# Splitting plain weight blocks with casting and accumulating DMAs in a two-layer trunk kernel

## The chip, the cores and the metric

The kernel is one program on one core of a Trainium2 chip. The engines named below are PE (matrix multiplication, and PEld, its weight loads), DVE (elementwise), ACT (elementwise with functions), POOL (elementwise, and a queue of DMAs of its own) and SP (which here only issues DMAs). The metric is the device time of one execution in microseconds; the median of three runs stands for a kernel.

## The reference

A stream of 512 latent tokens and 256 context tokens, 1024 wide, goes through two layers. Layer 0 mixes tokens with a bidirectional chunkwise mLSTM, layer 1 with windowed grouped-query attention. A squared-ReLU MLP of width 4096 follows each. All in float32:

```
u = modulate(rms_norm(h, norm_mix[i]), shift, scale)
y = mixer(u, uc, w_in, w_out)                 # mLSTM (i = 0) or windowed attention (i = 1)
h = h + gate * y
h = h + gate2 * (square(relu(modulate(rms_norm(h, norm_ffn[i]), ...) @ w1[i])) @ w2[i])
return rms_norm(h, final_norm)
```

The context stream runs through layer 0 in full, and in layer 1 only as keys and values. Shifts, scales and gates come from a product of the conditioning vector with a 1024 by 6144 matrix in each layer.

## The kernel before

**Products.** TensorE gets float32 operands in its reduced type fp32r, so each operand is split into a high part (the operand cast to fp32r) and a low part (the operand less its high part). A product takes three matmuls, `mm3` at lines 96 to 98: high by high, low by high, high by low.

**Weight units.** Weights come as units of 128 by 1024 numbers (512 KB). A *plain* unit is a block as it lies in memory. `unit` (lines 73 to 87) loads it on SP's queue into one of three buffers `raw` (line 80), and `split` makes ACT cast it to `whi` (line 887) and DVE subtract to get `wlo` (line 888). `whi` and `wlo` have four buffers each, so a new unit can be split once the unit four before it has had its last matmul. I call the time from that last matmul to the first matmul of the new unit the unit's *lead*. The load lies before the lead, since `raw` is separate; the cast and the subtraction lie in it. In `dense_steps` each unit is asked for by `take`, which keeps two ahead; elsewhere `feed` takes the next of a planned list, and `take` and `feed` are placed by hand in the code of each stage.

**Stages,** in order of time: a start of some 50 us (loads, the first norms, the conditioning product), layer 0's mixer (to about 540 us; weights wg, wqk, wv, wo, wout, all plain), layer 0's MLP `ffn0` (540 to 920 us), layer 1's attention (920 to 1130 us; wskv, wsq, wsout, plain) and layer 1's MLP `ffn1` (1130 us to the end).

- `ffn0` multiplies two row blocks of w1 with halves of the tokens by a scheme of seven products instead of eight. Its w1 blocks are not plain: `pair_w1` loads two into `raw` (lines 986, 987), and POOL makes sums of them, four instructions on lines 994 to 997, which are then cast and subtracted. In `seven`, POOL also squares one result (line 1085) and adds two others (line 1088, `addg`). After each group of such products, `back` multiplies with w2, whose units (`w2a`) are plain: four to a chunk, in each of seven chunks.
- `ffn1` takes plain w1 units and forms its second product by a seven-product scheme over 2 by 2 groups of w2 blocks (`plan1`, lines 1180 to 1245): the blocks stay in tiles `wb`, and 28 subtractions on DVE (`less`, line 1208) form the sums of blocks that the scheme wants. These sums are split by the ACT cast and DVE subtraction of `split`.

The sequence on each engine is not the order of the code: a scheduler in the compiler orders the instructions of all engines by its own estimates, and the engines then run what they are given strictly in that order. A DMA issued on POOL's queue stands in POOL's order among its sums and squares: an entry that waits holds up all behind it.

POOL issues no DMA in the kernel before.

Of the kernel before, what the change touches and what calls it, by code (L numbers as in the profile page):

```python
# [9 lines left out]
F32 = mybir.dt.float32  # L10
F32R = mybir.dt.float32r
BF16 = mybir.dt.bfloat16
AF = mybir.ActivationFunctionType
ALU = mybir.AluOpType
# [7 lines left out]
P = 128  # L22
D = 1024
KT = D // P
NL = 512
# [31 lines left out]
class Trunk:  # L57
# [14 lines left out]

    def unit(self, src, eng=None):

        nc = self.nc
        if len(src.shape) == 3:
            src = src.rearrange("m p c -> p m c")
        n = int(np.prod(src.shape[1:]))
        raw = self.ring.tile([P, D], F32, name="raw", tag="raw", bufs=self.nraw)[:, :n]
        nc.sync.dma_start(out=raw if len(src.shape) == 2 else raw.rearrange("p (m c) -> p m c", m=src.shape[1]), in_=src)  # L80
        hi = self.ring.tile([P, D], F32R, name="whi", tag="whi", bufs=self.nsplit)[:, :n]
        lo = self.ring.tile([P, D], F32R, name="wlo", tag="wlo", bufs=self.nsplit)[:, :n]
        self.split(raw, hi, lo, eng)
        if self.ada_cap and self.ada_todo and self.ada_todo[0][:2] < self.ada_cap:
            self.ada_step()
        return hi, lo
# [1103 lines left out]
    def plan1(self):  # L1190

        nc, a = self.nc, self.a
        self.steps1 = [(0, 4), (8, 4), (16, 4), (24, 2)]
        self.w2r = w2r = {}
        at = 0

        def load(b, u, n):
            def f():  # L1200
                t = w2r[b, u] = self.fp.tile([P, D], F32, name=f"wb{b}", tag=f"w{b}{u}")
                nc.sync.dma_start(out=t, in_=a["w2b"][n])
            return f

        def less(o, x, y, u):

            def f():
                nc.vector.tensor_tensor(out=w2r[o, u], in0=w2r[x, u], in1=w2r[y, u], op=ALU.subtract)
            return f

        def w1(m, *extra):
            def f():
                r = self.unit(a["w1"][1, m])
                for x in extra:
                    x()
                return r
            return f

        def w2(b, u, *extra):
            def f():  # L1220
                hi, lo = [self.ring.tile([P, D], F32R, name=n, tag=n, bufs=self.nsplit) for n in ("whi", "wlo")]
                self.split(w2r[b, u], hi, lo)
                for x in extra:
                    x()
                return hi, lo
            return f
        self.plan, self.begun = [], []
        for base, nk in self.steps1:
            us = range(nk // 2)
            extra = []  # L1230
            for b in (12, 22, 11, 21):
                extra += [load(b, u, at + (11, 12, 21, 22).index(b) * len(us) + u) for u in us]
            extra += [less(12, 12, 11, u) for u in us]
            at += 4 * len(us)
            ms = [base + nk * i + k for k in range(nk) for i in range(2)]
            skip = 0 if base else 2
            per = -(-len(extra) // (len(ms) - skip))
            self.plan += [w1(m) for m in ms[:skip]]
            self.plan += [w1(m, *extra[per * i:per * i + per]) for i, m in enumerate(ms[skip:])]
            self.plan += [w2(b, u) for b in (11, 21) for u in us]  # L1240
            self.plan += [w2(22, u, less(22, 22, 12, u)) for u in us]
            self.plan += [w2(12, u, less(11, 22, 11, u)) for u in us]
            self.plan += [w2(22, u, less(21, 22, 21, u)) for u in us]
            self.plan += [w2(b, u) for b in (11, 21) for u in us]
        self.last1 = base + 2 * nk

        def w2_plain(i):

            def f():
                raw = self.ring.tile([P, D], F32, name="raw", tag="raw", bufs=self.nraw)  # L1250
                nc.sync.dma_start(out=raw, in_=a["w2l"][i])
                nc.vector.tensor_tensor(out=raw, in0=raw, in1=self.grow, op=ALU.mult)
                hi, lo = [self.ring.tile([P, D], F32R, name=n, tag=n, bufs=self.nsplit) for n in ("whi", "wlo")]
                self.split(raw, hi, lo)
                return hi, lo
            return f
        self.plan += [w1(m) for m in range(self.last1, 4 * KT)]
        self.plan += [w2_plain(i) for i in range(4 * KT - self.last1)]

    def ffn1(self, u, out):  # L1260

        nc, tc, a = self.nc, self.tc, self.a
        xs = self.xs(u)
        fp = self.fp
        H = NL // 2
        tt = nc.vector.tensor_tensor
# [27 lines left out]
        def two(name, k):  # L1294
            t = fp.tile([P, 2, NL], F32R, name=name, tag=f"{name}{k}")
            return t[:, 0, :], t[:, 1, :]
# [10 lines left out]
        def second(m, m0, k):  # L1307

            r0, r1, s34 = rt.pop(m0), rt.pop(m), rt.pop(("34", k))
            hid["12", k] = two("h12", k)  # L1310
            self.split(r1, *hid["12", k])
            s = fp.tile([P, NL], F32, name="s12", tag="s12", bufs=2)
            tt(out=s[:, 0:H], in0=r0[:, H:NL], in1=r1[:, H:NL], op=ALU.add)
            tt(out=s[:, H:NL], in0=s[:, 0:H], in1=r0[:, 0:H], op=ALU.subtract)
            tt(out=s34[:, H:NL], in0=r1[:, 0:H], in1=s[:, H:NL], op=ALU.subtract)
            for n, src in (("1", s), ("3", s34)):
                hid[n, k] = two("e" + n, k)
                self.split(src, *hid[n, k])
# [38 lines left out]
        for c, (base, nk) in enumerate(self.steps1):  # L1357
            for k in range(nk):
                m0, m1 = base + k, base + nk + k
                if c + k == 0:  # L1360
                    hidden([0, nk, 1, nk + 1], square, (("A", (0, 1)), ("A", (2, 3)), ("B", range(4))))
                if m0 not in rt:
                    hidden([m0], square)
                first(m0, k)
                if m1 not in rt:
                    hidden([m1], square)
                second(m1, m0, k)
            for p, n in ((1, "11"), (2, "12"), (3, "S4"), (5, "S1"), (6, "S2"), (7, "S3"), (4, "22")):
                if c == len(self.steps1) - 1 and p == 6:
                    self.rows1()  # L1370
                product(p, n, nk, c)
# [14 lines left out]
        def join(i):  # L1386
            a1, a3, a4, a5, a6 = [acc[p, i] for p in (1, 3, 4, 5, 6)]
            x = fp.tile([P, NL], F32, name="r", tag="r", bufs=4)
            for o, l, r, op in ((a6, a1, a6, ALU.add), (a1, kept[2, i], a1, ALU.add), (x, kept[7, i], a6, ALU.add),
                                (a6, a6, a5, ALU.add), (a3, a3, a6, ALU.add), (a4, x, a4, ALU.subtract),  # L1390
                                (a5, x, a5, ALU.add)):
                tt(out=o, in0=l, in1=r, op=op)
            for t, d, o in ((i, 0, a1), (i, 1, a3), (2 + i, 0, a4), (2 + i, 1, a5)):
                tt(out=o, in0=o, in1=self.grow[:, d * 512:(d + 1) * 512], op=ALU.mult)
                y = res[t][:, d * 512:(d + 1) * 512]
                tt(out=y, in0=y, in1=o, op=ALU.add)
        hp = []
        for n, m in enumerate(range(self.last1, 4 * KT)):
            hidden([m], square)
            hp.append(two("h12", n))  # L1400
            self.split(rt.pop(m), *hp[n])
            turn((0, 2, 1, 3)[n])
            if n % 2:
                join(n // 2)
# [3 lines left out]
        for t in (0, 2, 1, 3):  # L1408
            sv = ss[:, 3 * t:3 * t + 3]
            os = [None, None]  # L1410
            for d in range(2):
# [5 lines left out]
                y = res[t][:, ds]  # L1417
                tt(out=y, in0=ps, in1=y, op=ALU.add)
                nc.scalar.activation(out=junk[d], in_=y, func=AF.Square, accum_out=sv[:, d:d + 1])
                o = os[d] = fp.tile([P, NL], F32, name="r", tag="r", bufs=4)  # L1420
# [584 lines left out]
```

## Time and profile before

| | |
|---|---|
| median of three runs | 1549.54 us (1549.34 to 1550.19) |
| the profiled execution, its whole time | 1551.29 us |
| its span, first to last instruction | 1549.4 us |
| busy: PE, DVE, ACT, POOL | 1509.6, 1127.1, 740.2, 326.5 us |
| moved by DMA | 157.27 MB |
| mean granted TensorE clock | 0.992 |

The page gives busy time, share of the span and number of instructions for each engine, groups of equal instructions with their mean duration, and for each kind of DMA the median time from issue to landing. A row of a timeline is start, duration, engine, line, operation, output and input names, and in brackets the idle time before it with what ended that. In a row of windows come the window, its length, the busy time (and count) of PE, PEld, DVE, ACT and POOL, the granted clock, the share of time that DMA engines worked, and GB/s. The names whi, wlo, raw are those of the unit; mm, p, pb, pc, pj, kept and acc are PE's results; h and r are the MLP's activations.

### The profile page before, as it was taken

The page shows a single profiled execution, that of the slowest core. Times are in us where ns is not written, and L with a number is a line of the kernel's source. Part 1 is how long each engine was busy: PE and PEld are TensorE (multiplying, and loading weights), DVE is VectorE, ACT ScalarE, POOL GpSimd, SP SyncE. Part 2 cuts the span into 40 slices and gives each one's busy share as a digit, 9 for nine tenths or more (in the row PEclk, how much of TensorE's full clock was granted, in tenths as well). Part 3 has the DMA queues.
Part 4 walks back from the last instruction along what each step waited for, and adds up shares of the span by engine and source line. Part 5 has one row for each costly group of instructions (what it writes and reads, how often), then busy time and mean ns, then how long its engine had stood idle before and what let it go on. Part 6 is the DMA issues. An engine that isn't in the chain of part 4 may idle for free.

```text
span 1549.4 us, 23838 instructions
## 1 busy us (share of the span) xinstructions
PE 1509.6 (97%) x9110; PEld 1355.9 (88%) x9110; DVE 1127.1 (73%) x2084; ACT 740.2 (48%) x1501; POOL 326.5 (21%) x318
## 2 busy tenths in 40 slices
PE   6999999999999999999999999999999999999998
PEld 4778888878889999999999999888887988888886
DVE  3684657488797888767676667778888875757697
ACT  4533343344573332524424355666666665545454
POOL 0322111113203222232224221243443100000000
PEclk8999999999999999999999999999999999999999
DMA  8422323234231343343443422011111424150321
GB/s 316 139 83 69 125 82 118 73 116 150 74 110 42 120 139 124 125 146 125 148 145 100 150 69 66 32 34 42 42 41 43 177 83 149 41 163 28 109 69 55
DMA packets 47848, 157.27 MB, mean 102 GB/s; under 512 B 5327, under 2 KB 8911, under 8 KB 47607
## 3 DMA queue, kind: packets, MB, share of 16 engines
q1 hardware_dynamic: 46560, 154.25, 30.3%
q8 instruction: 72, 1.18, 0.3%
q10 hardware_dynamic: 1175, 1.51, 0.3%
q14 instruction: 41, 0.34, 0.1%
HBM read 153.64 MB, written 2.10 MB: 101 GB/s over the span
## 4 chain that ended last, share of the span: by engine, by line
PE 79%; DVE 6%; issue 4%; ACT 4%; POOL 3%; DMA 1%; POOLq 0%; DVEq 0%; ACTq 0%
PE mm L96 17%; PE mm L97 16%; PE mm L98 16%; PE p L98 2%; PE p L97 2%; PE p L96 2%; PE pt L1825 2%; PE pj L96 1%; PE pj L97 1%; PE pj L98 1%; PE at L843 1%; DVE adap L262 1%; PE av L1840 1%; ACT whi L887 1%; DVE wlo L888 1%
## 5 line engine op out<-in xcount | busy, mean ns | idle before, releaser
L888 DVE TENSOR_TENSOR wlo<-raw,whi 128x1024 fp32r<-128x1024 f32 (+2 forms) x152 | 179.6, 1186 | 82.3 <-ACT whi L887 80.6
L887 ACT CAST whi<-raw 128x1024 fp32r<-128x1024 f32 (+2 forms) x155 | 154.0, 999 | 141.9 <-PE mm L97 77.4
L96 PE MATMUL mm<-uH,whi 128*128 128x512 f32 (+1 forms) x496 | 189.4, 386 | 0.0
L97 PE MATMUL mm<-uL,whi 128*128 128x512 f32 (+1 forms) x496 | 186.7, 378 | 0.7 <-DVE uL L332 0.4
L98 PE MATMUL mm<-uH,wlo 128*128 128x512 f32 (+1 forms) x496 | 186.9, 378 | 0.0
L262 DVE SCALAR_TENSOR_TENSOR adap<-raw,crow 128x1024 bf16<-128x1024 f32 x128 | 165.8, 1295 | 19.9 <-DMA raw<-ada 19.1
L96 PE MATMUL mm<-h,whi 128*128 128x384 f32 x512 | 172.9, 338 | 1.9 <-ACT h L887 1.9
L97 PE MATMUL mm<-h,whi 128*128 128x384 f32 x512 | 172.6, 337 | 0.5 <-DVE h L888 0.5
L98 PE MATMUL mm<-h,wlo 128*128 128x384 f32 x512 | 172.1, 336 | 0.0
L887 ACT CAST whi<-sum 128x512 fp32r<-128x512 f32 (+1 forms) x42 | 31.9, 761 | 165.8 <-PE mm L97 75.9
L98 PEld LDWEIGHTS mm<-uH,wlo 128*128 128x128 f32 x496 | 93.4, 188 | 17.9 <-issue 0.9
L97 PEld LDWEIGHTS mm<-uL,whi 128*128 128x128 f32 x496 | 93.6, 189 | 16.4 <-DVE uL L489 0.7
L96 PEld LDWEIGHTS mm<-uH,whi 128*128 128x128 f32 x496 | 92.9, 189 | 15.6 <-issue 0.3
L96 PEld LDWEIGHTS mm<-h,whi 128*128 128x128 f32 x512 | 96.1, 188 | 2.8 <-ACT h L887 2.8
L97 PEld LDWEIGHTS mm<-h,whi 128*128 128x128 f32 x512 | 96.1, 188 | 1.5 <-DVE h L888 1.4
L98 PEld LDWEIGHTS mm<-h,wlo 128*128 128x128 f32 x512 | 96.1, 188 | 0.0
L888 DVE TENSOR_TENSOR wlo<-wb,whi 128x1024 fp32r<-128x1024 f32 x49 | 59.2, 1221 | 35.9 <-ACT whi L887 35.8
L888 DVE TENSOR_TENSOR h<-r,h 128x384 fp32r<-128x384 f32 (+2 forms) x100 | 56.4, 568 | 34.1 <-ACT h L887 33.8
L887 ACT CAST whi<-wb 128x1024 fp32r<-128x1024 f32 x49 | 51.6, 1054 | 60.9 <-PE mm L97 27.1
L1809 POOL TENSOR_SCALAR e<-e,den 128x512 f32<-128x512 f32 (+1 forms) x64 | 49.0, 779 | 135.1 <-DVE den L1807 86.9
L98 PE MATMUL p<-t,wlo 128*128 128x384 f32 x224 | 75.4, 337 | 0.5 <-DVE wlo L888 0.5
L97 PE MATMUL p<-t,whi 128*128 128x384 f32 x224 | 75.2, 336 | 0.0
(401 smaller groups left out, 4180.0 us busy)
## 6 DMA issues: line engine op xcount, KB each, us to landing
raw<-ada SPq DMA_DIRECT2D x80, 512.0 KB, 3.6
raw<-w SPq DMA_DIRECT2D x64, 512.0 KB, 3.5
raw<-w2a SPq DMA_DIRECT2D x32, 512.0 KB, 3.5
wb<-w2b SPq DMA_DIRECT2D x28, 512.0 KB, 4.2
adaw<-ada SPq DMA_DIRECT2D x16, 512.0 KB, 7.7
hL<-xT SPq DMA_DIRECT2D x16, 256.0 KB, 3.5
raw<-wqk SPq DMA_DIRECT2D x8, 512.0 KB, 4.0
raw<-wv SPq DMA_DIRECT2D x8, 512.0 KB, 3.5
```

What stands on the lines that cost most here:

```text
L96: mm(out=out, lhsT=ah, rhs=bh, start=start, stop=False)
L97: mm(out=out, lhsT=ah, rhs=bl, start=False, stop=False)
L98: mm(out=out, lhsT=al, rhs=bh, start=False, stop=stop)
L262: self.tc.keep_in_program_order(nc.vector.scalar_tensor_tensor(out=pr, in0=w, scalar=0.5, in1=self.crow[:, v, :], op0=ALU.mult, op1=ALU.mu ...
L843: mm(out=o[hh][:, i * VW:(i + 1) * VW], lhsT=pw[g, d, hh][:, i, :], rhs=v[:, 3 * g + i, hh, :], start=False, stop=i == 2)
L887: keep(self.nc.scalar.copy(out=hi, in_=src))
L888: keep((eng or self.nc.vector).tensor_tensor(out=lo, in0=src, in1=hi.bitcast(F32), op=ALU.subtract))
L1809: nc.gpsimd.tensor_scalar(out=out[ii][:, :W], in0=out[ii][:, :W], scalar1=den[:, ii:ii + 1], scalar2=1.0, op0=ALU.mult, op1=ALU.mult)
L1825: nc.tensor.transpose(out=pt[:, i * P:(i + 1) * P], in_=ps_[i][:, n * P:(n + 1) * P], identity=self.ident)
L1840: mm(out=o, lhsT=vv, rhs=ph, start=n == 0, stop=False)
```

## The change

`unit` no longer loads into `raw`. A DMA on POOL's queue reads the block from memory and casts it into `whi` on its way (line 86 of the changed kernel). ACT then writes minus `whi` into `wlo` (line 87). A second DMA on POOL's queue reads the same block again and adds it onto `wlo` (line 89), which leaves block less high part. This holds for 129 blocks in 123 calls (a wout unit of three or four blocks is loaded in as many pieces, and two such calls lie among them); the split of sums and of activations stays as it was, now on lines 893 and 894. The sum `less` on DVE becomes `more`, an accumulating DMA on POOL's queue (line 1214); since a DMA adds and does not subtract, `plan1` forms other sums, loads one block again (7 more loads on SP), and the activations and results that go with them change sign. The rest of the lines moves down: 96 to 98 become 102 to 104, 994 to 997 become 1000 to 1003, 1085 and 1088 become 1091 and 1094.

```diff
     def unit(self, src, eng=None):
...
-        raw = self.ring.tile([P, D], F32, name="raw", tag="raw", bufs=self.nraw)[:, :n]
-        nc.sync.dma_start(out=raw if len(src.shape) == 2 else raw.rearrange("p (m c) -> p m c", m=src.shape[1]), in_=src)
-        hi = self.ring.tile([P, D], F32R, name="whi", tag="whi", bufs=self.nsplit)[:, :n]
-        lo = self.ring.tile([P, D], F32R, name="wlo", tag="wlo", bufs=self.nsplit)[:, :n]
-        self.split(raw, hi, lo, eng)
+        hi, lo = [self.ring.tile([P, D], F32R, name=t, tag=t, bufs=self.nsplit)[:, :n] for t in ("whi", "wlo")]
+        def parts(t):
+            return [(t, src)] if len(src.shape) == 2 else [
+                (t[:, i * src.shape[2]:(i + 1) * src.shape[2]], src[:, i, :]) for i in range(src.shape[1])]
+        for t, s in parts(hi):
+            nc.gpsimd.dma_start(out=t, in_=s)
+        nc.scalar.activation(out=lo, in_=hi.bitcast(F32), func=AF.Copy, scale=-1.0)
+        for t, s in parts(lo):
+            nc.gpsimd.dma_start(out=t, in_=s, accum_op=ALU.add)
...
-        def less(o, x, y, u):
+        def more(o, x, u, n=None):
             def f():
-                nc.vector.tensor_tensor(out=w2r[o, u], in0=w2r[x, u], in1=w2r[y, u], op=ALU.subtract)
+                nc.gpsimd.dma_start(out=w2r[o, u], in_=w2r[x, u] if n is None else a["w2b"][n], accum_op=ALU.add)
...
-            for b in (12, 22, 11, 21):
-                extra += [load(b, u, at + (11, 12, 21, 22).index(b) * len(us) + u) for u in us]
-            extra += [less(12, 12, 11, u) for u in us]
+            for b in (11, 12, 21, 22):
+                extra += [load(b, u, block(b, u)) for u in us]
+            extra += [more(12, 11, u) for u in us]
...
-            self.plan += [w2(b, u) for b in (11, 21) for u in us]
-            self.plan += [w2(22, u, less(22, 22, 12, u)) for u in us]
-            self.plan += [w2(12, u, less(11, 22, 11, u)) for u in us]
-            self.plan += [w2(22, u, less(21, 22, 21, u)) for u in us]
+            self.plan += [w2(11, u, load(11, u, block(12, u)), more(11, 22, u, block(22, u))) for u in us]
+            self.plan += [w2(21, u) for u in us]
+            self.plan += [w2(22, u, more(22, 12, u)) for u in us]
+            self.plan += [w2(12, u) for u in us]
+            self.plan += [w2(22, u, more(21, 22, u)) for u in us]
```

Two places show how the order of instructions moves. The first is POOL in the middle of layer 0's MLP, in one chunk: from the square that belongs to the last products before `back` (a tensor_tensor on r by r) to the addition. Before:

```order
L1085 TENSOR_TENSOR r_7523<-r_7523 128x384
L994 TENSOR_TENSOR sum1_7563<-raw_7555 128x512
L996 TENSOR_TENSOR sum0_7562<-raw_7554,raw_7555 128x512
L995 TENSOR_TENSOR sum0_7562<-sum1_7563,raw_7554 128x512
L997 TENSOR_TENSOR sum1_7563<-raw_7554,sum0_7562 128x512
L1088 TENSOR_TENSOR r_7525<-r_7522,r_7524 128x384
L1085 TENSOR_TENSOR r_7675<-r_7675 128x384
L1088 TENSOR_TENSOR r_7677<-r_7674,r_7676 128x384
```

The same stretch of POOL in the changed kernel, where whi and wlo of w2a are the chunk's plain units:

```order
L86 DMA whi_6481<-w2a 128x1024
L1091 TENSOR_TENSOR r_6450<-r_6450 128x384
L1000 TENSOR_TENSOR sum1_6656<-raw_6648 128x512
L1002 TENSOR_TENSOR sum0_6655<-raw_6647,raw_6648 128x512
L1001 TENSOR_TENSOR sum0_6655<-sum1_6656,raw_6647 128x512
L1003 TENSOR_TENSOR sum1_6656<-raw_6647,sum0_6655 128x512
L86 DMA whi_6519<-w2a 128x1024
L89 DMA wlo_6482<-w2a 128x1024
L1094 TENSOR_TENSOR r_6452<-r_6449,r_6451 128x384
L86 DMA whi_6579<-w2a 128x1024
L89 DMA wlo_6520<-w2a 128x1024
```

The last two rows of the part before are the same square and addition as the changed part's r_6450 and r_6452: nothing stood between them. Now the four sums for the next pair of w1 blocks stand there, behind them the accumulating DMA of the chunk's first w2a unit (wlo_6482), and the addition of line 1094 behind that DMA.

The second place is a change from w2 sums back to plain w1 units in layer 1's MLP. ACT there before (whi from wb are splits of w2 blocks, whi from raw those of plain w1 units):

```order
L887 CAST whi_14358<-wb21_13838 128x1024
L887 CAST whi_14362<-wb21_13840 128x1024
L887 CAST whi_14392<-raw_14390 128x1024
L887 CAST whi_14402<-raw_14400 128x1024
L887 CAST whi_14440<-raw_14438 128x1024
L887 CAST whi_14450<-raw_14448 128x1024
L887 CAST whi_14488<-raw_14486 128x1024
```

ACT and then POOL at that place in the changed kernel:

```order
L893 CAST whi_13655<-wb21_13196 128x1024
L1360 COPY acc_13653<-mm_13640 128x512
L893 CAST whi_13659<-wb21_13198 128x1024
L87 ACTIVATE wlo_13690<-whi_13689 128x1024
L1360 COPY acc_13720<-mm_13707 128x512
L87 ACTIVATE wlo_13699<-whi_13698 128x1024
```

```order
L1214 DMA wb12_13705<-wb11_13696 128x1024
L86 DMA whi_13689<-w1 128x1024
L86 DMA whi_13698<-w1 128x1024
L89 DMA wlo_13690<-w1 128x1024
L86 DMA whi_13737<-w1 128x1024
L89 DMA wlo_13699<-w1 128x1024
```

Where one cast followed the next on ACT, each negation of ACT now stands between two DMAs of POOL, and waits for the first of them; results that ACT copies out of PE's buffers (line 1360) stand behind it.

More of the change, by code (lines that the diff above doesn't have):

```diff
@@ L1230, in plan1, with block @@
             extra = []
-            for b in (12, 22, 11, 21):
-                extra += [load(b, u, at + (11, 12, 21, 22).index(b) * len(us) + u) for u in us]
-            extra += [less(12, 12, 11, u) for u in us]
+            def block(b, u, at=at, n=len(us)):
+                return at + (11, 12, 21, 22).index(b) * n + u
+            for b in (11, 12, 21, 22):
+                extra += [load(b, u, block(b, u)) for u in us]
+            extra += [more(12, 11, u) for u in us]
             at += 4 * len(us)
@@ L1312, in second @@
             s = fp.tile([P, NL], F32, name="s12", tag="s12", bufs=2)
-            tt(out=s[:, 0:H], in0=r0[:, H:NL], in1=r1[:, H:NL], op=ALU.add)
+            tt(out=s[:, 0:H], in0=r0[:, H:NL], in1=r1[:, H:NL], op=ALU.subtract)
             tt(out=s[:, H:NL], in0=s[:, 0:H], in1=r0[:, 0:H], op=ALU.subtract)
-            tt(out=s34[:, H:NL], in0=r1[:, 0:H], in1=s[:, H:NL], op=ALU.subtract)
+            tt(out=s34[:, H:NL], in0=r1[:, 0:H], in1=s[:, H:NL], op=ALU.add)
             for n, src in (("1", s), ("3", s34)):
@@ L1389, in join @@
             for o, l, r, op in ((a6, a1, a6, ALU.add), (a1, kept[2, i], a1, ALU.add), (x, kept[7, i], a6, ALU.add),
-                                (a6, a6, a5, ALU.add), (a3, a3, a6, ALU.add), (a4, x, a4, ALU.subtract),
-                                (a5, x, a5, ALU.add)):
+                                (a3, a3, a5, ALU.add), (a3, a3, a6, ALU.subtract), (a4, x, a4, ALU.add),
+                                (a5, a5, x, ALU.subtract)):
                 tt(out=o, in0=l, in1=r, op=op)
```

## The prediction

> **What bounds the kernel now.** I read the busy times, then PE's busy time by stage, then what its waits are, then the ring of units stage by stage.
>
> The page's busy times, and the windows of the stages (start, length, busy PE, PEld, DVE, ACT, POOL, clock, DMA share, GB/s):
>
> ```profile
> PE 1509.6 (97%) x9110; PEld 1355.9 (88%) x9110; DVE 1127.1 (73%) x2084; ACT 740.2 (48%) x1501; POOL 326.5 (21%) x318
> ...
> 0.00:50.00 50.00, 38.20 (x226) 26.40 (x226) 21.86 (x50) 20.90 (x38) 2.05 (x7) 0.90 0.85 308
> 50.00:540.00 490.00, 484.36 (x3241) 428.86 (x3241) 344.57 (x680) 214.50 (x534) 108.69 (x98) 1.00 0.30 96
> 540.00:920.00 380.00, 377.12 (x2151) 375.19 (x2151) 276.91 (x477) 144.34 (x247) 108.40 (x74) 1.00 0.40 129
> 920.00:1130.00 210.00, 202.56 (x1453) 183.70 (x1452) 168.78 (x396) 132.08 (x306) 71.92 (x91) 0.98 0.14 45
> 1130.00:1500.00 370.00, 364.79 (x1848) 306.78 (x1847) 277.04 (x420) 205.66 (x333) 33.30 (x44) 1.00 0.28 91
> 1500.00:1549.00 49.00, 42.53 (x203) 34.95 (x201) 37.92 (x64) 22.67 (x44) 2.18 (x4) 0.96 0.16 61
> ```
>
> PE sets the time. It idles 11.8 us in the first 50, 6.5 in the last 49, and between them 5.6 + 2.9 + 7.4 + 5.2 = 21.2 us. The change removes no matmul. So whatever it takes from DVE, no more than some 21 us can come of it; and whatever delays a unit beyond its lead is added in full, as PE has no slack to give it back.
>
> **What the change removes.** The rows by group (busy, mean ns, then idle before and its releaser):
>
> ```profile
> L888 DVE TENSOR_TENSOR wlo<-raw,whi 128x1024 fp32r<-128x1024 f32 x130 | 162.4, 1254 | 76.9 <-ACT whi L887 75.2 <-PE mm L1382 1.0
> L887 ACT CAST whi<-raw 128x1024 fp32r<-128x1024 f32 x133 | 138.7, 1049 | 127.4 <-PE mm L97 74.1 <-PE mm L98 14.0 <-PE kept L98 10.7
> ...
> L1208 DVE TENSOR_TENSOR wb<-wb,wb 128x1024 f32<-128x1024 f32 x28 | 33.6, 1220 | 2.4 <-DMA wb<-w2b 2.3
> ```
>
> Some 120 of the 130 subtractions go (the rest split w1 blocks of `pair_w1`), 120 x 1.25 = 150 us, and 28 x 1.22 = 34 us of `less`: 184 of DVE's 1127 us. ACT keeps one instruction a unit, of about the same 1.05 us. What does DVE's relief give PE? PE's longest waits, in total, count and longest:
>
> ```profile
> PE at L382 <- DVE sq L380: 7.4, 1, 7.4
> PE s L1778 <- ACT e L1798: 2.2, 3, 0.8
> PE at L308 <- DVE ssL L295: 2.1, 1, 2.1
> PE acc L96 <- ACT uH L419: 2.0, 2, 1.7
> PE mm L96 <- ACT y L1655: 2.0, 1, 2.0
> PE mm L96 <- ACT h L887: 1.9, 2, 1.7
> PE at L751 <- DVE kp L764: 1.8, 2, 1.1
> ```
>
> The 7.4 belongs to the first norm, which no unit is split before. Of the rest few end on DVE. I credit 4 us (0 at the least, 12 at the most).
>
> **What it adds: a chain inside the lead.** Before, the lead held a cast and a subtraction, 1.05 + 1.25 = 2.3 us. Now it holds a DMA into `whi`, a negation, and a second DMA onto `wlo`; neither DMA can start before the slot is free. The trace has no DMA from POOL's queue, no casting and no accumulating one. The nearest rows are SP's loads of the same 512 KB (KB, median us from issue to landing):
>
> ```profile
> raw<-w SPq DMA_DIRECT2D x64, 512.0 KB, 3.5
> ...
> wb<-w2b SPq DMA_DIRECT2D x28, 512.0 KB, 4.2
> adaw<-ada SPq DMA_DIRECT2D x16, 512.0 KB, 7.7
> ...
> crow<-ccr SPq DMA_DIRECT2D x1, 1024.0 KB, 7.4
> ```
>
> Low end: 3.5 each, so 3.5 + 1.05 + 3.5 = 8.05 us. High end: 7.7 each, as where SP's loads crowd each other, or as an accumulation that costs like a load of twice the bytes (7.4 for 1 MB): 16.5. I take 4.5 each, just above the rows for loads among others (3.5 to 4.2), because the two readings double the traffic and POOL has to make the request: 4.5 + 1.05 + 4.5 = 10 us. That is the estimate on which the sum hangs most.
>
> [...]
>
> Bandwidth itself is no bound: 123 units read twice add some 63 MB, and the sums some 18 more (28 accumulations and 7 loads of 0.52 MB), to 157 MB before, about 239 in all; over 1550 us that is 154 GB/s against 308 in the first window.
>
> **Where the lead is short.** A matmul takes 0.174 us at 384 columns (50 us for 288) and 0.225 at 512 (50 for 222):
>
> ```profile
> 500.00:550.00 50.00, 50.00 (x288) 50.00 (x287) 41.96 (x70) 19.35 (x33) 10.63 (x6) 1.00 0.38 120
> ...
> 1300.00:1350.00 50.00, 50.00 (x223) 41.39 (x222) 34.26 (x49) 29.15 (x42) 0.00 (x0) 1.00 0.16 53
> ```
>
> With these I count matmuls, in the changed order, from the end of a slot's old unit to the first use of the new `wlo`. In layer 0's mixer most leads are 18 to 31 us: nothing is lost. Shorter ones, in us: the first wv 6.4; wout 10.3 (but in pieces, four DMAs each way); wskv 12.4 falling to 7.4; the first wsq 5.1 and 4.5; the first w1 units of layer 0's MLP 8.4 and 8.8; the first units of layer 1's MLP 6.8, 6.8 and 5.4; each return from w2 to w1 there 7.6.
>
> *Layer 0's MLP*, the largest term. PE, DVE and POOL in one chunk before, in order of time:
>
> ```profile
> 569.48 0.34 PE L96 MATMUL p<-t,whi 128*128 128x384 f32 x1
> ...
> 570.77 0.68 DVE L888 TENSOR_TENSOR wlo<-raw,whi 128x512 fp32r<-128x512 f32 x1
> ...
> 576.39 1.18 POOL L1085 TENSOR_TENSOR r<-r 128x384 f32<-128x384 f32 x1 [10.38 <-ACT r L1083]
> ...
> 580.30 0.33 PE L98 MATMUL mm<-h,wlo 128*128 128x384 f32 x1
> ```
>
> The slot of the chunk's first w2a unit is free at 569.5, and its `wlo` wanted at 580.3, a lead of 10.8 us. In the changed order of POOL its accumulating DMA stands behind the square (which ended at 577.6, 8.1 us into the lead) and behind two to four of the sums. Those are
>
> ```profile
> L996 POOL TENSOR_TENSOR sum<-raw 128x512 f32<-128x512 f32 x14 | 25.4, 1817 | 54.1 <-DVE t L888 50.4 <-DVE wlo L888 3.7
> ...
> L994 POOL TENSOR_TENSOR sum<-raw 128x512 f32<-128x512 f32 x14 | 23.8, 1703 | 71.5 <-DMA raw<-w 69.9 <-DVE wlo L888 1.6
> ...
> L995 POOL TENSOR_TENSOR sum<-sum,raw 128x512 f32<-128x512 f32 x14 | 22.0, 1568 | 0.2
> ...
> L997 POOL TENSOR_TENSOR sum<-raw,sum 128x512 f32<-128x512 f32 x14 | 19.0, 1357 | 0.9
> ```
>
> together 6.4 us. Their data can be there: `raw` is free from 571.4, and a load issued then lands 3.5 us later, at 575. So the DMA is issued 10.7 us (two sums, 2.9) to 14.5 us (all four) into the lead, and lands 3.5 to 4.5 later, at 14.2 to 19.0, where 10.8 was wanted: PE waits 3.4 to 8.2 us. POOL's addition and ACT's work behind the next negation come late as well, but within the same wait. I take 5 us, nearer the low end, as the first of the later products can run meanwhile where the order lets it; six chunks have sums there: 30 us (20 to 49; 8 if the scheduler's picture of the time is the right one and the DMA gets out early).
>
> *Returns to w1 in layer 1's MLP*: ACT and PE at one of them,
>
> ```profile
> 1283.26 1.05 ACT L887 CAST whi<-raw 128x1024 fp32r<-128x1024 f32 x1 [2.54 <-PE kept L98]
> ...
> 1289.87 0.39 PE L96 MATMUL mm<-uH,whi 128*128 128x512 f32 x1
> ```
>
> The slot was free at 1283.26 and the unit wanted at 1289.87 (`whi`) and, with the four matmuls of 0.225 that now stand before the first use of `wlo`, at 1290.8: 7.5 us, about the count's 7.6, against 10. Wait 2.5, three times: 7.5 us (1.5 to 27).
>
> *Starts of stages*, 10 less the lead: wv 3.5, wskv 2.5, wsq 5.5; first w1 units 3 (1.6, and norm sums between the DMAs in POOL's order), wout 3 (more pieces), layer 1's MLP 7 (4.6, and norm sums again), the last chunk 1: 25.5 us (5 to 60).
>
> *Start of the kernel*: wg and wqk are now asked for first, on a queue of their own, beside loads that run at 308 GB/s; 1 MB at that rate is 3.4 us: 3 us (0 to 8).
>
> *POOL's queue in layer 1's attention*: each DMA that waits for a slot or a negation holds the normalisation behind it,
>
> ```profile
> L1809 POOL TENSOR_SCALAR e<-e,den 128x512 f32<-128x512 f32 (+1 forms) x64 | 49.0, 779 | 135.1 <-DVE den L1807 86.9
> ```
>
> 64 of them feed PE, and PE already waits there (the 2.2 us for `e`). For some 12 DMAs I take 0.5 us each: 6 us (0 to 15).
>
> The sum: 30 + 7.5 + 25.5 + 3 + 6 - 4 = 68 us. It stands on the profiled execution, 1551.3 us whole around its span of 1549.4, and that is 1.75 above the median: 1551.3 + 68 - 1.75 = 1618 us. All low ends (8 + 1.5 + 5 + 0 + 0, less 12) give +2.5, near 1552; all high ends (49 + 27 + 60 + 8 + 15) +159, near 1709.
>
> **Rivals.**
> - *DVE's relief decides.* If each DMA took 2.9 us or less (below every row above), the chain would be 6.8 us and fit nearly all leads; then PE's inner idle shrinks. Of 21.2 us perhaps 12: 1537 us. For: DVE is 73% busy, and ends some of PE's waits. Against: the leads of 4.5 to 6.8 us, and POOL's order in layer 0's MLP, which no faster DMA mends. [...] Chance 0.11.
> - *All is hidden.* The scheduler could have put DMAs early enough, and the relief pays for the few waits: 1550 us. 0.05.
> - *The DMAs are dear.* At 16.5 us a chain all leads below that stall: 6.5 more at six chunks (39), at three returns (20), at some ten units of stage starts (65): 1618 + 124 = 1742 us. [...] 0.17.
> - [...] 0.12.
>
> **How the numbers follow.** My forecast, waits by short leads with a chain near 10 us, has 0.55. Faster or slower means by more than 0.2% (3.1 us), which is what can be told from no change here. Faster 0.11; within 0.2% 0.05; slower 0.55 + 0.17 + 0.12 = 0.84. The range, 1545 to 1700, holds the forecast's cases and the port's, reaches into no change, and leaves out the faster rival and most of the dear one (0.2 in all).
>
> **What would show it.** PE busy stays near 1510 and DVE falls to about 943. New idle time of PE, 60 to 70 us, stands before matmuls that want `whi` or `wlo` and is ended by DMAs: some 30 us in layer 0's MLP in six like pieces, the rest at the places named, and almost none in layer 0's mixer. Some 239 MB are moved. The landing of a POOL DMA is 4 to 5 us. I am wrong if PE's idle time shrinks, if the landing is below 3 or above 7 us, if idle time in the MLP of layer 0 is spread over all its units, or if POOL's own time for a request, of which I know nothing, comes out as the bound.

## The result, and the profile after

The changed kernel takes 1829.54 us (1825.91 to 1832.30) against 1549.87 before: a ratio of 1.180, 95% interval 1.177 to 1.183. It is slower, as forecast, but by 280 us where 68 were forecast.

The changed kernel's page: busy times, and the bytes that moved.

```profile
PE 1579.7 (86%) x9110; PEld 1404.9 (77%) x9110; DVE 973.4 (53%) x1941; ACT 736.4 (40%) x1496; POOL 505.9 (28%) x601
...
DMA packets 71564, 239.10 MB, mean 131 GB/s; under 512 B 8048, under 2 KB 12656, under 8 KB 71320
```

The span is 1827.6 us. PE runs the same 9110 matmuls but is busy 1579.7 us, 70 more than before, and idle 248, 208 more. Both parts make the 278 us. DVE's busy time fell by 154 us, where 184 were forecast. To see where, the stages are cut at the same matmul counts (the 226th, 3464th, 5613th, 7064th) as the prediction's windows of before. The changed kernel's windows, with the same columns:

```profile
0.00:55.00 55.00, 36.22 (x226) 26.22 (x227) 19.45 (x51) 21.55 (x40) 8.17 (x15) 0.91 0.96 318
55.00:613.00 558.00, 503.26 (x3240) 443.05 (x3240) 297.18 (x637) 213.12 (x533) 165.41 (x193) 0.94 0.51 123
613.00:1049.00 436.00, 389.81 (x2152) 387.21 (x2151) 256.19 (x452) 144.48 (x247) 129.11 (x122) 0.95 0.52 141
1049.00:1287.00 238.00, 212.62 (x1451) 193.10 (x1450) 153.52 (x384) 129.92 (x301) 93.96 (x127) 0.93 0.35 76
1287.00:1777.00 490.00, 394.95 (x1848) 320.74 (x1847) 214.34 (x364) 203.71 (x331) 104.80 (x139) 0.90 0.61 141
```

Start +5 us, layer 0's mixer +68, its MLP +56, layer 1's attention +28, its MLP +120. The granted clock is below 1 in each, where it was 1.00 in three of them. The mixer, in which the prediction expected almost no idle time, has 55 us of it, against 6 before; the rest of its 68 us, 19, are slower matmuls.

PE's longest waits (us in all, times, longest) are now for units; one for ACT's state C in the mixer is shown beside them:

```profile
PE mm L104 <- DMA wlo<-w2a: 49.2, 8, 10.1
PE mm L104 <- DMA wlo<-w: 41.9, 15, 8.2
PE mm L102 <- DMA whi<-w: 40.7, 10, 12.6
PE mm L104 <- DMA wlo<-wout: 23.0, 6, 8.7
...
PE at L787 <- ACT C L815: 9.8, 3, 5.9
```

How the DMAs landed (KB, median us from the issue):

```profile
whi<-w2a POOLq DMA_DIRECT2D x32, 512.0 KB, 4.5
wlo<-w2a POOLq DMA_DIRECT2D x32, 512.0 KB, 5.6
```

And what POOL waited for longest:

```profile
POOL r L1091 <- ACT r L1089: 177.0, 8, 28.7
POOL wlo L89 <- issue: 156.3, 38, 7.9
POOL wlo L89 <- ACT wlo L87: 147.9, 37, 8.2
POOL whi L86 <- PE mm L104: 134.3, 30, 16.2
POOL wb L1214 <- issue: 56.2, 11, 5.9
POOL whi L86 <- issue: 47.2, 30, 5.1
```

For w2a a casting DMA lands after 4.5 us, as I took, and an accumulating one after 5.6; over the other units of 512 KB, wg's single one aside, the medians are 3.8 to 5.3 and 5.5 to 5.8. The rows with "issue" are new: 156 + 56 + 47 = 260 us in which POOL waited before a DMA for nothing that a semaphore tells. POOL's timeline, in one chunk of layer 0's MLP, shows them:

```profile
581.75 0.61 POOL L86 DMA_DIRECT2D whi<-w2a  x1
582.36 0.93 POOL L89 DMA_DIRECT2D wlo<-w2a  x1
582.94 1.38 POOL L1094 TENSOR_TENSOR r<-r 128x384 f32<-128x384 f32 x1
586.22 0.59 POOL L86 DMA_DIRECT2D whi<-w2a  x1 [1.89 <-issue]
588.76 0.86 POOL L89 DMA_DIRECT2D wlo<-w2a  x1 [1.95 <-ACT h L893]
590.98 0.56 POOL L86 DMA_DIRECT2D whi<-w2a  x1 [1.36 <-issue]
594.98 0.87 POOL L89 DMA_DIRECT2D wlo<-w2a  x1 [3.44 <-issue]
600.70 0.91 POOL L89 DMA_DIRECT2D wlo<-w2a  x1 [4.84 <-issue]
```

By the trace's landings the DMA issued at 581.75 landed at 585.91, and the next one starts at 586.22; that of 588.76 landed at 594.67, and one starts at 594.98; that of 594.98 landed at 600.38, and one starts at 600.70. Each starts 0.3 us after a landing. Over the whole run no accumulating DMA ever starts while another is in flight (0 of 157), though one casting DMA with one accumulating one, or three casting ones, are found together. So something had room for about that much, and a number in the kernel's set-up was the first suspect: `dynamic_dma_scratch_size=512`. I call it the store, of 512 bytes; what is kept in it, and how, no run shows.

### The profile page after: what moved, and what is told of

It is laid out like the page before. It is cut to its first block, busy times and chain, and to the rows that moved or that the text cites. A ratio compares the mean times of both kernels' runs of the same rounds, so it can differ in the third digit from the quotient of the medians.

```text
span 1827.6 us, 24045 instructions
## 1 busy us (share of the span) xinstructions
PE 1579.7 (86%) x9110; PEld 1404.9 (77%) x9110; DVE 973.4 (53%) x1941; ACT 736.4 (40%) x1496; POOL 505.9 (28%) x601
## 4 chain that ended last, share of the span: by engine, by line
PE 35%; issue 22%; DMA 15%; POOL 10%; ACT 6%; DVE 5%; POOLq 0%; SPq 0%; ACTq 0%; DVEq 0%
PE mm L104 9%; PE mm L102 8%; PE mm L103 8%; DMA whi<-w 3%; DMA wlo<-w2a 3%; POOL wlo L89 2%; DMA wb<-w2b 2%; DMA whi<-wsout 1%; POOL whi L86 1%; DMA wb<-wb 1%; DMA raw<-w 1%; ACT wlo L87 1%; PE pt L1835 1%; POOL wb L1214 1%; DMA wlo<-w 1%
## 5 line engine op out<-in xcount | busy, mean ns | idle before, releaser
L87 ACT ACTIVATE wlo<-whi 128x1024 fp32r<-128x1024 f32 (+1 forms) x123 | 128.2, 1044 | 360.9 <-DMA whi<-w 163.5
L102 PE MATMUL mm<-uH,whi 128*128 128x512 f32 (+1 forms) x496 | 198.9, 405 | 41.8 <-DMA whi<-w 40.7
L104 PE MATMUL mm<-uH,wlo 128*128 128x512 f32 (+1 forms) x496 | 193.2, 393 | 39.7 <-DMA wlo<-w 39.7
L104 PE MATMUL mm<-h,wlo 128*128 128x384 f32 x512 | 179.7, 351 | 49.2 <-DMA wlo<-w2a 49.2
L103 PE MATMUL mm<-uL,whi 128*128 128x512 f32 (+1 forms) x496 | 193.0, 391 | 0.8 <-DVE uL L338 0.7
L102 PE MATMUL mm<-h,whi 128*128 128x384 f32 x512 | 179.6, 351 | 4.6 <-ACT h L893 4.4
L103 PE MATMUL mm<-h,whi 128*128 128x384 f32 x512 | 178.1, 348 | 0.3 <-DVE h L894 0.2
L102 PEld LDWEIGHTS mm<-h,whi 128*128 128x128 f32 x512 | 101.1, 197 | 5.4 <-ACT h L893 4.9
L103 PEld LDWEIGHTS mm<-h,whi 128*128 128x128 f32 x512 | 101.2, 198 | 0.9 <-DVE h L894 0.9
L894 DVE TENSOR_TENSOR h<-r,h 128x384 fp32r<-128x384 f32 (+2 forms) x100 | 63.0, 634 | 70.4 <-ACT h L893 70.3
L104 PE MATMUL mm<-uC,wlo 128*128 128x256 f32 x208 | 62.7, 302 | 25.2 <-DMA wlo<-wout 23.0
L103 PE MATMUL p<-t,whi 128*128 128x384 f32 x224 | 75.2, 336 | 0.0
L102 PE MATMUL p<-t,whi 128*128 128x384 f32 x224 | 75.2, 336 | 0.0
```

Source lines behind the costliest of these rows:

```text
L87: nc.scalar.activation(out=lo, in_=hi.bitcast(F32), func=AF.Copy, scale=-1.0)
L102: mm(out=out, lhsT=ah, rhs=bh, start=start, stop=False)
L103: mm(out=out, lhsT=ah, rhs=bl, start=False, stop=False)
L104: mm(out=out, lhsT=al, rhs=bh, start=False, stop=stop)
L894: keep((eng or self.nc.vector).tensor_tensor(out=lo, in0=src, in1=hi.bitcast(F32), op=ALU.subtract))
```

## The experiments

Two theories stood at the start. The *lead theory* is the prediction's: two landings one behind the other do not fit the short leads. The *queue theory*: POOL's queue takes one accumulating DMA at a time, and holds POOL meanwhile.

**A larger store.**

```diff
-    nc = bacc.Bacc("TRN2", target_bir_lowering=False, num_devices=1, dynamic_dma_scratch_size=512)
+    nc = bacc.Bacc("TRN2", target_bir_lowering=False, num_devices=1, dynamic_dma_scratch_size=1024)
```

> [...] The queue theory: in the changed kernel POOL starts no accumulating DMA while another is in flight, and waits 260 us for that with no releaser in the profile (156 before wlo, 47 before whi, 56 before the sums); twice the store lets two of each be in flight, so most of these 260 us go and the time falls to 1640 to 1720 us. The lead theory (the two landings one behind the other are too long for the leads, whatever the queue does): the landings of 4.5 and 5.6 us stay, and the time stays at 1810 to 1840 us.

Measured: 1723.35 us, ratio 1.111 (1.108 to 1.114): 3 us above the queue theory's bounds, and far from the lead theory's. One number in the program's set-up takes 106 us off, and nothing else moved: by the two traces every engine runs the same operations on the same tiles in the same order. Of POOL's waits in that run, the longest and the longest on "issue":

```profile
POOL wlo L89 <- ACT wlo L87: 251.3, 63, 9.5
POOL r L1091 <- ACT r L1089: 206.4, 8, 33.5
POOL whi L86 <- PE mm L104: 146.1, 32, 17.4
...
POOL wb L1214 <- issue: 15.8, 9, 3.2
```

Of the waits on "issue" 16 us are left before sums, and 4 before whi and wlo. 81 of the 157 accumulating DMAs now start while another is in flight. By stage the gain is 4 us at the start, 25 in the mixer, 3 in layer 0's MLP, 9 in the attention, 68 in layer 1's MLP. The queue theory holds for these: with more store POOL's waits on "issue" fell from 260 to 20 us. The 173 us that remain it does not explain.

**Each part of the change alone.** In one run only `unit` is the changed one, in the other only the sums (`more`, the blocks' order, the signs; that a DMA does not subtract, for which the signs changed, is my premise, and no run tried it).

> Only the plain units are changed; layer 1's sums stay subtractions on DVE, and the seven blocks loaded again and the changed signs are undone with them. 28 accumulating DMAs leave POOL's queue, all after 1250 us. The queue theory: they hold the queue 5.5 us each, 28 x 5.5 = 154 us, of which a part lies on PE's path in layer 1's MLP: 1750 to 1790 us. The lead theory: the sums have long leads and cost nothing, only DVE's 34 us of subtractions come back: 1825 to 1840 us.

> Only layer 1's sums are changed to accumulating DMAs; plain units are loaded, cast and subtracted as before. Both theories: 28 DMAs of 5.5 us, 154 us of a queue in some 380 us, with little else on POOL there, are hidden: 1545 to 1565 us. If the sums are a cost of their own (a sum late for its split, as each product waits for the one before), 1570 us or more.

Units alone: 1778.84 us, 1.146 (1.144 to 1.149), within the queue theory's bounds. Without the sums layer 1's MLP loses 62 us and not 120. Sums alone: 1554.33 us, 1.0018 (1.0001 to 1.0035): as both theories had it, and nothing to speak of, although DVE is 29 us less busy.

```profile
PE 1511.9 (97%) x9110; PEld 1356.7 (87%) x9110; DVE 1098.4 (71%) x2056; ACT 739.2 (48%) x1501; POOL 352.3 (23%) x346
```

```profile
POOL wb L1208 <- issue: 60.1, 10, 9.3
```

The first is that run's row of busy times, the second one of POOL's waits. Here POOL waits 60 us on "issue" as well, and it costs little (the whole run is 0.0 to 0.4% slower): no plain unit is queued behind it. So the 58 us that the sums add to that stage in the changed kernel are not the sums' own; they come from what stands behind them. POOL's and PE's timeline there, in the changed kernel:

```profile
1597.90 0.88 POOL L1214 DMA_DIRECT2D wb<-wb  x1 [12.09 <-DMA wb<-w2b]
1603.82 0.89 POOL L1214 DMA_DIRECT2D wb<-wb  x1 [5.04 <-issue]
1604.43 0.85 POOL L86 DMA_DIRECT2D whi<-w  x1
1609.61 0.56 POOL L86 DMA_DIRECT2D whi<-w  x1 [4.34 <-issue]
...
1610.65 0.80 PE L102 MATMUL mm<-uH,whi 128*128 128x512 f32 x1 [12.64 <-DMA whi<-w]
```

A sum waits 12.1 us for a load by SP, the next sum 5.0 us on "issue", and only then is the casting DMA of the w1 unit issued that PE wants: PE stands still for 12.6 us. It is the second place of the order shown ahead of the prediction, where the sum stands above `whi` of w1.

**Casting without accumulating.** The high part comes by a casting DMA, the low part by SP's load and DVE's subtraction:

```diff
-        nc.scalar.activation(out=lo, in_=hi.bitcast(F32), func=AF.Copy, scale=-1.0)
-        for t, s in parts(lo):
-            nc.gpsimd.dma_start(out=t, in_=s, accum_op=ALU.add)
+        (eng or nc.vector).tensor_tensor(out=lo, in0=raw, in1=hi.bitcast(F32), op=ALU.subtract)
```

(with `raw` loaded as before the change, and the sums as before).

> Plain units with the casting DMA for the high part, but the low part by SP's load and DVE's subtraction as before (so ACT has no instruction a unit, and no DMA accumulates); layer 1's sums as before. The chain in the lead is one landing of 4.5 us and a subtraction of 1.25. The queue theory: up to three casting DMAs were in flight at once in the changed kernel, so nothing is held: 1555 to 1600 us, from the places with leads of 4.5 to 6 us only. The lead theory: a chain of 5.75 us against 11.2 loses about a fifth of what the change lost: 1600 to 1620 us. If any DMA of POOL's queue is dear, above 1650 us.

Measured: 1579.54 us, 1.018 (1.016 to 1.021), within the queue theory's bounds and below the lead theory's. It reads the blocks twice too (220.74 MB in all), so the double reading is not what costs: 30 us against 280. Layer 0's MLP, where the change lost 56 us, takes 379.2 us here and 379.9 before.

```profile
552.00:931.00 379.00, 376.81 (x2149) 374.72 (x2148) 287.35 (x479) 122.38 (x223) 115.77 (x98) 1.00 0.49 163
```

**Layer 0's MLP: POOL's order.** With the larger store that stage still lost 52 us. Now its sums, squares and additions leave POOL:

```diff
-                op = nc.gpsimd.tensor_tensor
+                op = nc.vector.tensor_tensor
...
-                         for e in (nc.vector, nc.gpsimd)]
+                         for e in (nc.vector, nc.vector)]
...
-            square(r11, nc.gpsimd)
+            square(r11, nc.vector)
```

> The kernel with the store of 1024 bytes (1723 us), and in layer 0's MLP the four sums, the square and the addition go from POOL to DVE, so that POOL has nothing but DMAs in that stage. There the doubled store gained only 3 of 56 us. The order theory: the accumulating DMA is late because it stands behind the square and the sums; without them it is issued when the negation is done, and lands 4.5 + 1.05 + 5.6 = 11.2 to 12.9 us after the slot is free, against 10.8 wanted, so the six waits of 5.4 to 8.9 us shrink to 0 to 2: 1670 to 1695 us. If the landings alone make the waits, or if DVE, with some 50 us more in this stage, becomes late itself: 1715 us or more.

Measured: 1686.85 us, 1.085 (1.082 to 1.088), within the order theory's bounds. PE's waits for w2a, with the larger store alone and with this:

```profile
PE mm L104 <- DMA wlo<-w2a: 49.5, 8, 8.9
```

```profile
PE mm L104 <- DMA wlo<-w2a: 19.6, 8, 5.0
```

The stage falls from 432 to 401 us. DVE is 21 us busier in it, and PE has no wait for DVE there. So 31 of the 52 us were the work that stood ahead of the DMAs in POOL's order. This work is also shorter on DVE (21 us there, 90 on POOL), and the run does not tell apart what that alone gave. The other 21 us are the waits of 1.2 to 5.0 us for wlo that remain, and slower matmuls; that they are the landings alone (5.1 and 5.8 us in the median there) was not tested.

**Long leads.** Only wqk, wv and wo of the mixer are split by DMAs:

```diff
+        if src.tensor.name not in ("wqk", "wv", "wo"):
+            (load, cast and subtraction as before)
+            return hi, lo
```

> Only the 24 units of wqk, wv and wo in layer 0's mixer are split by DMAs; wg, wout and all later units, and the sums, are as before; store of 512 bytes. Their leads were counted as 18 to 31 us but for the first wv (6.4). The lead theory: 1550 to 1558 us, the first wv's wait and nothing else, and no gain from 24 subtractions (30 us) less on DVE. If negations that wait on ACT hold back the mixer's own small operations (in the changed kernel PE waited 9.8 us for ACT's state C there), 1560 us or more. If DVE's relief is worth something, below 1546.

Measured: 1573.01 us, 1.012 (1.009 to 1.015): the case of 1560 us or more, and above what I expected. PE's longest waits that before did not have:

```profile
PE acc L113 <- DMA wlo<-wqk: 6.8, 1, 6.8
PE at L796 <- ACT C L824: 6.3, 1, 6.3
PE mm L112 <- DMA wlo<-wv: 4.7, 1, 4.7
```

All three end before 126 us, and the stages after the mixer keep their lengths within 1.1 us. The start lost 9.4 us and the mixer 12.7. The wait for ACT's state C is the case of the negation that holds back ACT: ACT stands still for 8.0 us before a wqk unit's negation, and the two copies into C come behind it. The other two are waits for landings in the first 90 us. So I took the same split for ten units only, six of wv and four of wo, all later than these:

> Ten units of layer 0's mixer alone are split by DMAs, six of wv and four of wo, all with leads of 18 us or more; wqk and the first two wv, at which the run with 24 units lost its 22 us (all of it before 125 us), are as before. Store of 512 bytes. The lead theory: nothing is late and nothing gained, 1548 to 1553 us. If a DMA split costs something even with an ample lead, 1555 us or more.

Measured: 1552.31 us, ratio 1.0004 (0.9985 to 1.0024): no change. The leads of these units, 18 us or more, hid the whole chain, and no gain from DVE's relief can be seen, which is only 12 us in this run.

**Store and units without sums.** Units alone with 1024 bytes:

> Only the plain units are changed, as in the run of 1779 us, with the store of 1024 bytes. If store and sums act apart: 1779 - 107 = 1672 us. If a good part of what the larger store gave lay in the sums and units that share the queue in layer 1's MLP (of the 107 us gained, 68 were there, 25 in layer 0's mixer, 9 in the attention): 1779 - 25 - 9 - 25 = some 1715 us.

Measured: 1715.74 us, 1.103 (1.100 to 1.107): the second case. With the larger store the sums cost 8 us (1723 against 1716), with the smaller one 51 (1830 against 1779): sums and units get in each other's way through the store.

**What adding costs.** The second DMA casts and does not add, with either store:

```diff
-            nc.gpsimd.dma_start(out=t, in_=s, accum_op=ALU.add)
+            nc.gpsimd.dma_start(out=t, in_=s)
```

> The changed kernel, store of 512 bytes, but the second DMA of a unit casts the block into wlo and adds nothing (so wlo holds the high part once more, the product is another one; the sums of layer 1 still add). The number and place of DMAs stay. The queue theory: an accumulating DMA fills the store, a casting one a third of it, so POOL is held much less, and the landing is 4.5 instead of 5.6 us: 1690 to 1740 us. If adding is no dearer for the queue than casting: 1815 to 1835 us.

> The kernel with the store of 1024 bytes (1723 us), in which the second DMA of a unit again casts the block into wlo and adds nothing (wlo holds the high part, the product is another one; the sums of layer 1 still add). With the larger store no wait of POOL before whi or wlo was left, so what adding still costs can only be its longer landing: 5.6 to 6.4 us against 3.9, some 2 us at each place where PE waits for a unit. If so, with some 24 such places and the matmuls at half clock behind them: 1650 to 1680 us, and 20 to 50 us below the same kernel with 512 bytes (1701), all of it in layer 1's MLP, where POOL waited 54 us for the store before sums. If adding had cost through the store alone: 1715 us or more.

Measured: 1701.44 us (1.094, 1.089 to 1.099) with 512 bytes and 1670.10 us (1.075, 1.071 to 1.079) with 1024. Landings without adding, 512 bytes:

```profile
whi<-w2a POOLq DMA_DIRECT2D x32, 512.0 KB, 4.4
wlo<-w2a POOLq DMA_DIRECT2D x32, 512.0 KB, 3.9
```

Both lie within the bounds given for the case that adding is dear. So at the same place a casting DMA lands 1.7 us sooner than an accumulating one (3.9 against 5.6); among the loads of wqk, in the mixer, it is only 0.2 (5.6 against 5.8). With the larger store, adding costs 1723 - 1670 = 53 us. POOL's waits on "issue" hardly differ with and without it (20 and 16 us), so this is the longer landing, the longer request (0.9 against 0.6 us in the changed kernel) and what follows from them. With the smaller store it costs 1830 - 1701 = 128 us. The store is worth 31 us where only the sums add, 25 of it in layer 1's MLP.

**The clock.** After its longer waits PE ran matmuls at half pace. With the larger store, the windows ahead of, over and behind one stretch in layer 0's MLP (the clock stands before the DMA share):

```profile
617.00:627.00 10.00, 6.64 (x39) 6.32 (x37) 3.37 (x7) 2.36 (x4) 7.74 (x8) 1.00 0.31 100
627.20:637.40 10.20, 5.20 (x16) 5.20 (x17) 3.57 (x7) 6.13 (x11) 3.37 (x5) 0.50 1.05 251
637.40:647.00 9.60, 9.60 (x56) 9.60 (x56) 5.88 (x11) 2.11 (x2) 0.90 (x1) 1.00 0.70 129
```

A wait of 8.6 us ends at 632.2; until 637.4 a matmul takes 0.32 us, 16 in 5.2, and then 0.17. In the changed kernel all 22 waits of PE of 3 us or more that began at full clock were followed by such a stretch within 3.5 us of their end, and so were 8 of 23 waits of 1 to 3 us. To tell a cause from a companion, I filled the waits:

```diff
+                    if 0 < c < NC - 1 and x == (0, 0) and ks == (0, 2):
+                        for _ in range(40):
+                            nc.tensor.matmul(out=pss[x], lhsT=hi[:, 0:P], rhs=hid[0][t][0], start=True, stop=True)
```

> The kernel with the store of 1024 bytes (1723 us), with 40 matmuls more before the first product of w2a in the six chunks of layer 0's MLP where PE waits 5.4 to 8.9 us for wlo. They compute nothing that is used; they need only the high part, which is there by then, and take 40 x 0.174 = 7 us of a wait. In that stage 52 us were lost, of which 41 in idle time and 11 in matmuls at half clock (44 us of the stage have a granted clock of 0.5, each time after such a wait). The clock theory (a wait of PE is followed by some 3 to 10 us at half clock, which is a cost beside the wait): the matmuls fill the waits, the clock stays at 1.0, and the stage gets shorter by some 5 to 10 us although work is added: 1712 to 1718 us. If the clock falls for another reason, the stage keeps its length or gets longer by the first chunk's 1.6 us: 1721 to 1727 us.

Measured: 1721.19 us, 1.110 (1.108 to 1.112). As a whole that can't be told from 1723, at the edge of what the second case had. The stage itself, cut at the same matmuls of the kernel, takes 427.8 us, not 432.4, although 200 of the 240 matmuls lie in it (the first chunk's 40 lie ahead of the cut). PE's waits there fall, and the same stretch of clock shrinks to 3.4 us:

```profile
637.00:640.50 3.50, 2.93 (x9) 2.94 (x10) 0.71 (x2) 2.18 (x5) 0.08 (x1) 0.51 0.96 234
```

The time at half clock in the stage falls from 44 to 10 us. So in this stage the waits brought the half clock about. What filling them is worth is less sure: 4.6 us there, less than the 5 to 10 expected, while the other stages are 0.9 to 2.6 us longer in this profile than in the one without the added matmuls. The stretches of half clock in the changed kernel's trace are 3.4 to 34 us long, multiples of 3.4 but for the last, which the end cuts off.

## Why the prediction was wrong, point by point

- **PE bounds, DVE's relief is worth little**: right as far as was tested. No gain can be seen where DVE has 29 us less (the sums alone) or 12 (ten units): ratios 1.0018 and 1.0004. The whole relief, which I credited with 4 us, was never tested without the DMAs.
- **The chain of 10 us**: nearly right by its parts, 4.5 + 1.05 + 5.6 = 11.2 by the changed kernel's landings. But from the issue of a unit's first DMA to the landing of its second it took 13.8 us in the median over all units (12.9 with the larger store), since waits lie between the two. I had the landings and not the queue between them.
- **"Neither DMA can start before the slot is free"** was the condition from which I took each wait, as 10 us less the lead; POOL's order came on top in layer 0's MLP, at the norm sums and in the attention. This is the step that failed. In the changed kernel a DMA on POOL's queue started when its slot was free (134 us of POOL's waits before `whi` were for PE's matmuls), when all ahead of it in POOL's order had run (the square on line 1091 alone waited 177 us for ACT), and when the store had room (260 us on "issue", and 20 with the larger store). The store I put at nothing: it is not in the prediction, and it cost 106 us, more than the whole sum of 68. The order I left out at the returns to w1. What I named as unknown, POOL's own time for a request, was small in the changed kernel: 0.6 us for a cast and 0.9 for an accumulation.
- **Layer 0's MLP, 30 us (20 to 49)**: the mechanism was right for the larger part, six waits behind square and sums, as the run with these on DVE shows. The size was off, 56: waits of 3.2 to 10.1 us where I said 3.4 to 8.2 and took 5, and 13 us of slower matmuls. (A slip in that reckoning, 10.7 for 8.1 + 2.9 = 11.0, changes little.)
- **Returns to w1 in layer 1's MLP, 7.5 us (1.5 to 27), and its start, 7**: 120 us. I took the lead from the matmuls and left out of account that the order which I showed has the sums ahead of `whi`: `whi` was issued late, and the cast, not the accumulation, was missing (12.6, 11.8 and 6.8 us at the three returns). With the larger store 52 us are left, which no run takes apart.
- **Long leads lose nothing**: right for ten late units. The first wqk units were in my sum only by the start's 3 us, and wv by 3.5; with 24 units the start and the mixer lost 22. A negation that waited 8.0 us for its DMA also held up ACT's other work there, and so PE waited for that work and not for the unit (the 6.3 us for C); this I had only for layer 0's MLP, and there within the same wait. In the changed kernel the mixer lost 68 where I had 6.5 (wv and wout): PE's waits there are 23 us for wout, 10 for C, 5 for wv and 17 for smaller ones.
- **wout, 3 us**: PE waited 23 us for it, and 11 with the larger store. With the smaller one its pieces queue one behind the other: four accumulations take four landings (issued at 420.5, 424.0, 427.8 and 431.2 us, each of the last three 0.3 us after the landing before).
- **Attention 14 us** (wskv, wsq, POOL's queue): 28, and 20 with the larger store.
- **The clock**: not in the prediction at all, although the windows that it quotes have 0.90, 0.96 and 0.98 where PE waits. PE's busy time rose by 70 of the 278 us for the same matmuls; of this busy time 148 us lie at half clock, against 20 before, and half of the difference is 64.
- **Rivals.** "Dear DMAs" gave 1742, nearest in size, by a wrong price, so the nearness is luck: it took 7.7 us a landing, and the medians by unit are 6.8 at the most. The 0.12 in the sum of chances ("the port's" in the range) stood for requests of POOL that wait for DVE. No run shows such a wait: of the 286 requests in the changed kernel none took longer than 0.97 us, an accumulating one took 0.89 us in the median while DVE ran and 0.88 while it did not, and with DVE busier in layer 0's MLP the time fell. Faster and no change were held unlikely and did not come.

The parts of the 280 us, one after the other: 106 by the store; then, each measured from the run of 1723 us, 53 by adding's longer landing and request, and 37 (31 of them in that stage) by POOL's work in layer 0's MLP. The last two were not taken away together, so that what is left, some 84 us, is a difference and not a measurement, and its cause stays open in part. Landings in short leads belong to it: the run in which only the high part comes by DMA still lost 30 us. No variant beat the kernel before: those that equal it split little or nothing that is urgent by DMA.

## What to carry to other kernels

Here DMAs that cast and add took 154 us of work off DVE and put 286 requests on POOL's queue. Price such a DMA by the whole way from the moment its buffer is free, through the queue's order and the room of its store, to its landing, and compare that with the time in which the result is wanted. Before giving POOL's queue work, look at how much store the program gives it (106 us here), and at what else stands in POOL's order (37 us here). In this kernel, with PE 97% busy, waits counted in full, and again as a slower clock behind them: 208 us more of idle time came with 70 us of slower matmuls.

## What was not expected of the hardware

- With the store of 512 bytes, POOL's queue never had two accumulating DMAs in flight (0 of 157 started so), and POOL stood still on "issue" for 260 us; with 1024, 81 of the 157 started while another was in flight, and 20 us of such waits were left.
- An accumulating DMA of 512 KB landed after 5.6 us, a casting one in its place after 3.9 (w2a, 512 bytes of store); in the changed kernel the request took POOL 0.9 us for an accumulating one, and 0.6 for a casting one.
- In the changed kernel each of the 22 waits of PE of 3 us or more that began at full clock was followed by a stretch at half clock; of 23 waits of 1 to 3 us it was 8.
- The page of the profile wrote these waits as "issue": no semaphore told of them, and only the landings of earlier DMAs gave them away (in the changed kernel all 49 accumulating DMAs that waited so started 0.3 us after a landing).
